# Weight products of three networks: one group of 512 tokens against two groups of 256 in the halves of a PSUM bank

## The chip, the cores and the metric

The kernel runs on one core of a Trainium2 chip. Its engines are TensorE (PE in the profile, with its weight loads as a row of their own, PEld), VectorE (DVE), ScalarE (ACT), GpSimd (POOL) and SyncE (SP), which issues most DMAs. The metric is the device time of one execution in microseconds, the median of several runs. The work is dense matrix products over 512 tokens, and nearly all of it stands on TensorE.

## The reference

Two transformer blocks follow each other on the same 512 tokens of 1,024 features. Between norms, attentions and gates stand three networks that this change touches:

```python
def swiglu(x, w1, w3, w2):
    return (jax.nn.silu(x @ w1) * (x @ w3)) @ w2
...
f = swiglu(rms_norm(h, ffn1_pre_g[l]), ffn1_w1[l], ffn1_w3[l], ffn1_w2[l])
h = h + 0.5 * rms_norm(f, ffn1_post_g[l])
...
f = swiglu(rms_norm(h, ffn2_pre_g[l]), ffn2_w1[l], ffn2_w3[l], ffn2_w2[l])
h = h + 0.5 * rms_norm(f, ffn2_post_g[l])
...
h2 = rmsnorm(x, g_mlp[i])
u = jax.nn.relu(jnp.einsum("bsd,df->bsf", h2, w_up[i]))
x = x + jnp.einsum("bsf,fd->bsd", u * u, w_down[i])
```

The first two have a hidden width of 2,816 (22 tiles of 128), the third of 4,096 (32 tiles). All values are float32.

## The kernel before, in words

Everything is held with features on the 128 partitions and tokens along the free dimension: a feature tile is 128 x 512, and `h` is eight of them. To keep float32 precision, every operand of a product is split into a rounded high part and the remainder, and one product of two tiles is three matmuls into the same PSUM bank: high x high, high x low, low x high (`mm3`, line 290 of the profile issues all of them). So each matmul comes with a weight load of its own (`LDWEIGHTS`), 128 x 128.

`lin` (line 296) makes one output tile: it takes a PSUM bank from a rotation of two pools (`lg` with three banks, `mm` with two), and runs over the k input tiles, three matmuls each, with a moving operand as wide as `tok`: 512 columns for all tokens, 256 for a half. `A` and `B` are the two halves of the tokens, `ALL` is both.

A network works in chunks of hidden tiles: 4, 4, 4, 4 and 6 in the two of 22 tiles (`ffn`), 6, 6, 6, 6 and 8 in the one of 32 (`mlp`). For each chunk it makes the hidden tiles ("up"), then adds their share to the eight output tiles ("down", `down` calls `stream`, which calls `lin`). The first chunk's ups are plain products: four or five are issued for half the tokens at a time while the norm before is still being finished (`begin`), the rest over all tokens (`stream`). The later chunks' ups go through `fast`: two output tiles by two halves of the tokens are got from seven products in place of eight, and each of those matmuls has 256 columns. The downs run over all 512 tokens, except the last few outputs of a network's last chunk, which are issued by halves (`tail` in `stream`).

Nobody writes the order of the instructions by hand: the framework's scheduler fixes it for each engine ahead of time, so where a product waits for an operand, matmuls of the next products stand between in TensorE's queue. At the end of a `fast` stretch the last of the seven products of the last pair (`last`) adds into a bank that VectorE has to read first (line 741 in `ffn`, line 1385 in `mlp`), so it stands behind the first matmuls of the down that follows. The last hidden tiles of a chunk reach the down through ScalarE (line 510, the high part) and VectorE (line 511, the low part).

Of the kernel before, what the change touches and what calls it, by code (L numbers as in the profile page):

```python
# [56 lines left out]
HALVES = (A, B)  # L57
ALL = slice(0, S)
# [116 lines left out]
def width(tok):  # L175
    return tok.stop - tok.start


class Net:
# [116 lines left out]
    def lin(self, wt, xs, tok=ALL, bank=None):  # L296

        out = (bank or self.pm)()[:, : width(tok)]
        for k, x in enumerate(xs):
            self.mm3(out, wt[k], (x[0][:, tok], x[1][:, tok]), k == 0, k == len(xs) - 1)  # L300
        return out

    def begin(self, jobs, step, fill=()):
# [1330 lines left out]
```

## Time and profile before

| | |
|---|---|
| median of 3 runs | 2098.67 us (2090.48 to 2103.62) |
| profiled execution, its own time | 2091.38 us |
| its span, first to last instruction | 2089.6 us |
| TensorE busy (share of the span), matmuls | 2011.4 us (96%), 12,428 |
| weight loads busy | 1766.1 us (85%) |
| VectorE, ScalarE, GpSimd busy | 1544.4, 1101.7, 254.4 us |
| mean granted TensorE clock | 0.99 of full speed |

How to read it: the ends of matmuls in a trace are modelled, and matmuls overlap in the pipeline, so a matmul of 256 columns shows a length of 276 ns or more while the next one starts 113 ns after it. What a matmul costs in a stream is therefore read from start to start: the start of one merged row of the timeline to the start of the next, divided by the number of matmuls in the first. Where a matmul waited, the timeline says so behind its row ("0.88 <-ACT b L510": idle for 0.88 us, released by the ScalarE instruction of line 510 that wrote a tile `b`).

### The profile page before, as it was taken

Reading aid. Unit: us, or ns where it says so; the run is one execution under the profiler, and the core shown is the slowest. Engines: PE = TensorE matmul, PEld = TensorE weight load, DVE = VectorE, ACT = ScalarE, POOL = GpSimd, SP = SyncE. Lnnn points to the kernel's source line nnn. Section 1 sums busy time; section 2 is a strip of 40 time slices with the busy share of each in tenths; the row PEclk is TensorE's granted clock in tenths of the full one; section 3 lists DMA queues with packets and bytes.
Section 4 is the critical chain, followed back from the end, with each engine's and each line's share of the span. In section 5 each row is a group of like instructions: output and inputs, shape, how many; then the busy total and the mean of one; then the engine's idle time right before and its main releaser. Section 6 shows DMA issues by size and latency. Waiting matters only on the chain. (4 is left out here: it accounts for less than half of the span.)

```text
span 2089.6 us, 32337 instructions
## 1 busy us (share of the span) xinstructions
PE 2011.4 (96%) x12428; PEld 1766.1 (85%) x12428; DVE 1544.4 (74%) x2956; ACT 1101.7 (53%) x2052; POOL 254.4 (12%) x239
## 2 busy tenths in 40 slices
PE   8999999899999999999999998998999999999997
PEld 7899998778778888998999998776778888988997
DVE  7977786799775585587777869588987678666755
ACT  5644454673573454554445445467864436444752
POOL 2000002313331310040000003213100000000001
PEclk9999999899999999999999999999999999999999
DMA  5233333212222233221333342211112313323331
GB/s 163 91 112 97 106 107 122 71 61 91 91 71 95 77 120 103 93 70 51 113 110 102 106 141 72 66 41 51 41 41 81 114 31 122 99 89 104 112 101 41
DMA packets 66010, 186.43 MB, mean 89 GB/s; under 512 B 6976, under 2 KB 14144, under 8 KB 65856
## 3 DMA queue, kind: packets, MB, share of 16 engines
q1 hardware_dynamic: 63376, 180.97, 26.8%
q10 hardware_dynamic: 2448, 3.41, 0.5%
q8 instruction: 97, 1.59, 0.3%
q14 instruction: 57, 0.47, 0.1%
q0 software_dynamic: 32, 0.00, 0.0%
HBM read 182.25 MB, written 2.10 MB: 88 GB/s over the span
## 5 line engine op out<-in xcount | busy, mean ns | idle before, releaser
L290 PE MATMUL mm<-x,w 128*128 128x512 f32 (+1 forms) x2064 | 473.8, 379 | 0.0
L290 PE MATMUL mm<-b,w 128*128 128x256 f32 (+1 forms) x2625 | 448.6, 322 | 2.0 <-ACT b L510 1.8
L290 PEld LDWEIGHTS mm<-x,w 128*128 128x128 f32 x2064 | 364.0, 188 | 74.9 <-DVE v L1274 0.7
L290 PEld LDWEIGHTS mm<-b,w 128*128 128x128 f32 x2625 | 375.2, 188 | 48.9 <-ACT b L510 4.2
L252 ACT CAST w<-r 128x1024 fp32r<-128x1024 f32 (+2 forms) x256 | 229.8, 898 | 277.8 <-PE mm L290 118.0
L290 PE MATMUL lg<-x,w 128*128 128x256 f32 (+1 forms) x2460 | 348.6, 295 | 6.8 <-DVE t L1385 4.7
L253 DVE TENSOR_TENSOR w<-r,w 128x1024 fp32r<-128x1024 f32 (+2 forms) x254 | 267.8, 1055 | 116.3 <-ACT w L252 111.3
L290 PE MATMUL lg<-b,w 128*128 128x256 f32 (+1 forms) x1929 | 352.9, 334 | 0.0
L290 PEld LDWEIGHTS lg<-x,w 128*128 128x128 f32 x2460 | 315.9, 188 | 27.9 <-DVE t L1385 6.4
L290 PEld LDWEIGHTS lg<-b,w 128*128 128x128 f32 x1929 | 294.5, 188 | 42.1
L457 ACT CAST w<-r 128x1024 fp32r<-128x1024 f32 x147 | 154.6, 1053 | 138.1 <-PE lg L290 81.3
L458 DVE TENSOR_TENSOR w<-r,w 128x1024 fp32r<-128x1024 f32 x147 | 178.7, 1221 | 19.9 <-ACT w L457 19.4
L290 PE MATMUL mm<-x,u 128*128 128x256 f32 x756 | 108.1, 287 | 15.6 <-ACT x L513 7.1
L510 ACT CAST b<-t 128x512 fp32r<-128x512 f32 (+1 forms) x113 | 60.8, 539 | 112.5 <-DVE t L745 34.3
L290 PEld LDWEIGHTS mm<-x,u 128*128 128x128 f32 x756 | 96.9, 193 | 18.7 <-ACT x L513 7.5
L569 POOL TENSOR_TENSOR sh<-sh,sh 128x256 f32<-128x256 f32 x45 | 37.5, 834 | 502.8 <-ACT sh L563 499.9
L511 DVE TENSOR_TENSOR b<-t,b 128x512 fp32r<-128x512 f32 (+1 forms) x113 | 67.2, 596 | 26.3 <-ACT b L510 26.0
L569 POOL TENSOR_TENSOR sf<-sf,sf 128x256 f32<-128x256 f32 x28 | 23.3, 833 | 450.4 <-ACT sf L563 440.4
L563 ACT ACTIVATE sh<-h 128x256 f32<-128x256 f32 x128 | 49.9, 411 | 52.5 <-DVE h L630 22.7
L928 POOL TENSOR_TENSOR b<-b,rows 128x512 f32<-128x512 f32 x32 | 52.5, 1642 | 174.7 <-ACT b L926 174.7
L861 DVE TENSOR_TENSOR u<-tt,u 128x512 fp32r<-128x512 f32 x92 | 62.0, 684 | 9.9 <-ACT u L860 9.3
L290 PE MATMUL lg<-x,b 128*128 128x256 f32 x456 | 68.1, 291 | 0.0
(271 smaller groups left out, 2738.9 us busy)
## 6 DMA issues: line engine op xcount, KB each, us to landing
r<-in_ffn_w SPq DMA_DIRECT2D x86, 512.0 KB, 3.3
r<-in_w_in SPq DMA_DIRECT2D x64, 512.0 KB, 3.2
r<-in_ffn_w SPq DMA_DIRECT2D x68, 256.0 KB, 2.7
r<-in_w_up SPq DMA_DIRECT2D x32, 512.0 KB, 3.2
r<-in_w_down SPq DMA_DIRECT2D x32, 384.0 KB, 3.4
r<-in_ffn_w SPq DMA_DIRECT2D x16, 384.0 KB, 3.3
r<-in_w_out SPq DMA_DIRECT2D x8, 512.0 KB, 3.2
r<-in_xattn_w_k SPq DMA_DIRECT2D x8, 512.0 KB, 3.2
```

What stands on the lines that cost most here:

```text
L252: nc.scalar.copy(hi, raw)
L253: self.second.tensor_tensor(lo, raw, hi.bitcast(F32), op=OP.subtract)
L290: self.nc.tensor.matmul(ps, lhsT=lhsT, rhs=rhs, start=start, stop=stop, skip_group_check=on)
L457: nc.scalar.copy(hi, raw)
L458: nc.vector.tensor_tensor(lo, raw, hi.bitcast(F32), op=OP.subtract)
L510: nc.scalar.copy(hi, src)
L511: nc.vector.tensor_tensor(lo, src, hi.bitcast(F32), op=OP.subtract)
L563: nc.scalar.activation(t, x, AF.Square)
L569: eng.tensor_tensor(ts[0], ts[0], t, op=OP.add)
L861: nc.vector.tensor_tensor(lo, ps[:, :n], hi.bitcast(F32), op=OP.subtract)
L928: nc.gpsimd.tensor_tensor(t[:, tok], t[:, tok], r[:, tok], op=OP.mult)
```

## The change

`lin` looks whether it is called for all tokens within one of the three networks. If so it makes its output as two groups, one after the other: all k input tiles for tokens 0 to 255 into the first half of the bank, then all k tiles again for tokens 256 to 511 into the second half. The weights of each tile are loaded for each half. What reads the bank afterwards still reads all 512 columns at once. Everything else, attention and projections included, stays as it was.

```diff
     def lin(self, wt, xs, tok=ALL, bank=None):
 
         out = (bank or self.pm)()[:, : width(tok)]
-        for k, x in enumerate(xs):
-            self.mm3(out, wt[k], (x[0][:, tok], x[1][:, tok]), k == 0, k == len(xs) - 1)
+
+        halves = tok == ALL and self.phase in ("ffn1", "ffn2", "mlp")
+        for at in HALVES if halves else (tok,):
+            ps = out[:, at] if halves else out
+            for k, x in enumerate(xs):
+                self.mm3(ps, wt[k], (x[0][:, at], x[1][:, at]), k == 0, k == len(xs) - 1)
         return out
```

TensorE's queue has 12,146 rows before and 13,952 after. The scheduler sets the new matmuls in other places, and two of them matter.

The first place is TensorE's queue at the change from `fast` to the first down behind it in `mlp`. `mm_19060` (after: `mm_20314`) is the bank of the down's first output, the tiles `b` are parts of hidden tiles and `w` the weights, `lg_18929` (after: `lg_20183`) is the bank of the last `fast` product, which waits for VectorE. Before:

```order
L290 MATMUL lg_18929<-x_18568,w_18926 128x256
L290 MATMUL mm_19060<-b_18636,w_19055 128x512 [waits DVE_49]
L290 MATMUL mm_19060<-b_18637,w_19055 128x512
L290 MATMUL mm_19060<-b_18636,w_19056 128x512 [waits DVE_49]
L290 MATMUL mm_19060<-b_18638,w_19055 128x512
L290 MATMUL mm_19060<-b_18639,w_19055 128x512
L290 MATMUL mm_19060<-b_18638,w_19056 128x512
L290 MATMUL mm_19060<-b_18642,w_19055 128x512
L290 MATMUL lg_18929<-x_18507,w_18925 128x256 [waits DVE_49]
```

And with the change:

```order
L290 MATMUL lg_20183<-x_19786,w_20180 128x256
L290 MATMUL mm_20314<-b_19890,w_20309 128x256 [waits DVE_49]
L290 MATMUL mm_20314<-b_19891,w_20309 128x256
L290 MATMUL mm_20314<-b_19890,w_20310 128x256
L290 MATMUL mm_20314<-b_19892,w_20309 128x256
L290 MATMUL mm_20314<-b_19893,w_20309 128x256
L290 MATMUL lg_20183<-x_19689,w_20179 128x256 [waits DVE_49]
```

Seven matmuls of 512 columns stood ahead of the product that waits, now five of 256 do. There are eleven more such places. At eight of them the numbers are three of 512 before and five of 256 now; in the last chunk of each `ffn` four and seven; in that of `mlp` five and ten.

The second place is TensorE's queue at the first down of the first network, where the fourth hidden tile comes late. `mm_745` (after: `mm_841`) is the first output's bank, `b_157` and `b_158` are the high and low part of that tile. Before:

```order
L290 MATMUL mm_745<-b_153,w_740 128x512 [waits Activation_49]
L290 MATMUL mm_745<-b_154,w_740 128x512 [waits DVE_49]
L290 MATMUL mm_745<-b_153,w_741 128x512
L290 MATMUL mm_745<-b_157,w_740 128x512 [waits Activation_49]
L290 MATMUL lg_772<-b_145,w_767 128x512
```

And with the change:

```order
L290 MATMUL lg_880<-b_149,w_876 128x256
L290 MATMUL lg_880<-b_153,w_875 128x256
L290 MATMUL lg_880<-b_154,w_875 128x256
L290 MATMUL mm_841<-b_157,w_836 128x256 [waits Activation_49]
L290 MATMUL lg_880<-b_153,w_876 128x256
```

Nine matmuls of 512 columns of this down stood ahead of the wait for `b_157`; now seventeen of 256 do, nine of the first output's first half and eight of the second output's.

## Rows read from the trace of the kernel before

**Rows 1.** The page's first lines: busy time and share of the span by engine, and the granted TensorE clock in 40 slices of the span (tenths, 9 is 90% or more).

```profile
PE 2011.4 (96%) x12428; PEld 1766.1 (85%) x12428; DVE 1544.4 (74%) x2956; ACT 1101.7 (53%) x2052; POOL 254.4 (12%) x239
...
PEclk9999999899999999999999999999999999999999
```

**Rows 2.** What TensorE waited for in the first network (37 to 352 us), then in the third (1650 to 2030 us): the waiting line, the releaser, us in total, times, longest.

```profile
PE mm L290 <- ACT b L510: 0.9, 1, 0.9
PE lg L290 <- DVE t L741: 0.5, 1, 0.5
PE lg L290 <- ACT sh L474: 0.5, 1, 0.5
...
PE lg L290 <- DVE t L1385: 4.7, 4, 2.0
```

**Rows 3.** Timeline of TensorE in a down of the first network, 512 columns a matmul, 12 matmuls an output tile: start, us, engine, line, operation, count.

```profile
188.50 2.96 PE L290 MATMUL mm<-b,w 128*128 128x512 f32 x12
191.29 2.96 PE L290 MATMUL lg<-b,w 128*128 128x512 f32 x12
194.09 2.96 PE L290 MATMUL mm<-b,w 128*128 128x512 f32 x12
196.90 2.96 PE L290 MATMUL lg<-b,w 128*128 128x512 f32 x12
```

**Rows 4.** Timeline of TensorE over the first `fast` stretch of the first network, 256 columns a matmul, and the start of the down behind it; between the first row and the row at 119.95 us stand 312 matmuls.

```profile
84.59 2.88 PE L290 MATMUL mm<-b,w 128*128 128x256 f32 x24
87.31 1.52 PE L290 MATMUL lg<-x,w 128*128 128x256 f32 x12
...
118.59 1.52 PE L290 MATMUL lg<-x,w 128*128 128x256 f32 x12
119.95 0.85 PE L290 MATMUL mm<-b,w 128*128 128x512 f32 x3
120.64 1.67 PE L290 MATMUL lg<-x,w 128*128 128x256 f32 x12
```

**Rows 5.** The same view of a `fast` stretch of the third network; between the first row and the last one's start stand 144 matmuls.

```profile
1810.99 1.58 PE L290 MATMUL lg<-b,w 128*128 128x256 f32 x12
1812.41 2.99 PE L290 MATMUL mm<-b,w 128*128 128x256 f32 x24
...
1827.95 1.58 PE L290 MATMUL mm<-x,u 128*128 128x256 f32 x12
```

**Rows 6.** TensorE in the twelve `fast` stretches of the three networks, each from its first matmul to the first of the down behind it: us, busy us and matmuls (one or two that began just before are counted with each), granted clock, DMA share, GB/s. The stretches hold 324, 324, 324 and 492 matmuls of their own in each of the first two networks, and 240, 240, 240 and 324 in the third, 3,972 in all.

```profile
83.23:119.95 36.72, 36.72 (x325) 1.00 0.39 123
143.93:181.31 37.38, 37.28 (x326) 1.00 0.35 108
205.30:242.32 37.02, 37.02 (x325) 1.00 0.35 108
266.28:323.72 57.44, 56.79 (x494) 1.00 0.37 115
985.88:1022.60 36.72, 36.72 (x325) 1.00 0.43 136
1046.59:1084.74 38.15, 38.15 (x325) 1.00 0.33 105
1108.69:1145.69 37.00, 37.00 (x326) 1.00 0.34 109
1169.66:1226.99 57.33, 56.81 (x493) 1.00 0.36 115
1737.71:1764.92 27.21, 27.21 (x242) 1.00 0.49 154
1802.32:1830.78 28.46, 28.46 (x241) 1.00 0.37 116
1866.47:1893.94 27.47, 27.47 (x242) 1.00 0.36 117
1930.32:1967.31 36.99, 36.99 (x326) 1.00 0.31 96
sum 457.89, PE 456.62; mean PE 38.05
```

**Rows 7.** Timeline of TensorE where the first `fast` stretch of `mlp` ends and its down begins.

```profile
1764.92 1.78 PE L290 MATMUL mm<-b,w 128*128 128x512 f32 x7
1768.67 1.65 PE L290 MATMUL lg<-x,w 128*128 128x256 f32 x12 [1.97 <-DVE t L1385]
```

**Rows 8.** Timeline at the first down of the first network: the nine matmuls ahead of the wait, the ScalarE cast that they wait for, and the matmul that waited.

```profile
59.69 2.26 PE L290 MATMUL mm<-b,w 128*128 128x512 f32 x9
...
62.15 0.62 ACT L510 CAST b<-t 128x512 fp32r<-128x512 f32 x1 [1.88 <-POOL t L719]
...
62.82 0.50 PE L290 MATMUL mm<-b,w 128*128 128x512 f32 x1 [0.88 <-ACT b L510]
```

**Rows 9.** The page's DMA queues: those that carry instructions (packets, MB, share of 16 engines' span).

```profile
q8 instruction: 97, 1.59, 0.3%
q14 instruction: 57, 0.47, 0.1%
```

## The prediction

> **What bounds the kernel now.** I read the busy line of the page first: TensorE is busy for 96% of the span, VectorE for 74%, and the granted clock is at its upper level, 2.4 GHz, in all 40 slices [rows 1]. That busy share is modelled, so the next view is the list of what TensorE waited for inside the networks: 1.9 us in the first and 4.7 us in the third [rows 2]. TensorE's own stream is the bound there; what the change is worth is the time that a matmul takes from start to start, times their number, and what happens to those few waits. The third view is therefore the timeline, read from start to start.
>
> With 512 columns, a down of 12 matmuls per output goes 188.50, 191.29, 194.09, 196.90: 8.40 us for 36, **233.3 ns each** [rows 3]. With 256 columns there are two paces. In the first `fast` stretch 312 matmuls take 119.95 - 84.59 = 35.36 us, **113.3 ns each** [rows 4]; in a stretch of the third network 144 take 1827.95 - 1810.99 = 16.96 us, **117.8 ns each** [rows 5]. Both hold for many groups on end at the full clock, with the same sources and banks. The row of stretches tells how they mix: 27.47 us for 240 matmuls is 114.5 ns, 28.46 us for 240 is 118.6, and over all twelve it is 456.62 busy us for 3,972, **115.0 ns** [rows 6]. Two halves thus cost 226.6 ns at the one pace, 235.6 at the other and 230.0 in the mean, against 233.3 for the whole. Cutting a matmul in two is nearly free here, and that is the point of the case: the whole matmul of 512 columns carries more than twice what half a one does.
>
> **How many.** In each `ffn` the down has 8 outputs x 22 tiles x 3 = 528 matmuls, less those that were issued by halves already: 5 x 6 x 3 = 90 in the first, 4 x 6 x 3 = 72 in the second, so 438 and 456. The plain ups over all tokens are 8 jobs less the 4 or 5 begun by halves: 4 and 3 jobs x 24 = 96 and 72. In `mlp` the down has 8 x 32 x 3 = 768 less 3 x 8 x 3 = 72, so 696, and 2 ups x 24 = 48. Together 1,806, which is by how much TensorE's queue grows (13,952 - 12,146), so the change does what it says. They fill 1,806 x 233.3 ns = 421 us, a fifth of the span.
>
> **The sum.** *Pace.* 1,806 x (230.0 - 233.3) ns = -6.0 us. The ends are 1,806 x (226.6 - 233.3) = -12.1 us if all go at the fast pace, and 1,806 x (235.6 - 233.3) = +4.2 us at the slow one. I take the mean of the stretches since they use the same tiles and weights in the same networks, and are what the new streams run on from. The weight loads double with the matmuls, but they have run once per 256 columns in those stretches already, so their price is inside the pace. So is that of fetching more instructions; the queues that carry them use 0.4% of the DMA engines [rows 9], and 3,612 instructions on top of 2 x 12,428 of TensorE's [rows 1] do not change that.
>
> That first pace is where a rule and the trace part. The Trainium skill, "TensorE: Matmul & The Clock Gate", section "Back-to-back issue gap", gives the gap between isolated matmuls at full clock as N/2.4 ns plus a fixed 2.5 ns. By it a whole matmul would cost 215.8 ns, a half 109.2, and a pair 2.5 ns more than a whole: +4.5 us, an estimate from that page. The rows above show a larger gap for both, and not the same addition to each, so I keep to them.
>
> *What the rows do not show.* No matmul of 256 columns in these rows is known to write the second half of a bank. Both ends for it are again the two paces; I see no reason for a third.
>
> *Cover ahead of waits.* The scheduler put fewer microseconds ahead of the product that waits for VectorE at the end of a `fast` stretch. In the first down behind `fast` in `mlp` seven matmuls of 512 (1.63 us) stood there, and still the product waited 1.97 us [rows 7]; now five of 256 stand there (0.57 us). VectorE's end does not move, so the 1.06 us of work that was under the wait comes after it: **+1.1 us**. At two more places in `mlp`, and three in each `ffn`, it is three of 512 (0.70 us) against five of 256 (0.57), in the last chunk of each `ffn` four (0.93) against seven (0.80), in that of `mlp` five (1.17) against ten (1.14). In the first stretch the product starts 0.69 us after the three began [rows 4], so the wait ends about when the cover does, and the loss is at most 0.13 each: 10 x 0.13 + 0.03 = **+1.3 us**, or nothing where VectorE is early. At the first down of the first network nine of 512 (2.1 us) stood ahead of the wait for ScalarE, which lasted 0.88 us [rows 8]; now seventeen of 256 (1.95 us) do, so about +0.15 us, and as much in the second. Sum +2.7 us; the lower end is the 1.1 us alone. I take 2.5.
>
> *What costs nothing.* The bank is read once for all 512 columns as before, so VectorE and ScalarE do the same work. An output still takes 12 matmuls' worth of time (2.8 us) or more, the time in which its bank is read and the next weights are split. SP's and POOL's queues are unchanged in order. If that cover were gone, each of the 120 downs would wait for its weights; rows 2 has no such wait now, and TensorE gains only 0.04 us per output of 12.
>
> Together -6.0 + 2.5 = **-3.5 us**: from the profiled execution's own 2091.4 us to 2087.9. The median of the runs shown is 2098.7, 7.3 us above that execution, and the three runs lie 13 us apart. From the median the same step gives 2095.2. I put the forecast between the two, at **2091 us**.
>
> **The rivals.**
>
> *All at the fast pace.* If the long streams without a change of width stay at 113.3 ns, the pace gives -12.1 and with the 2.5 us it is -9.6: 2081.8 by the profile. For it: seven of the twelve stretches lie within 1.3 ns of it [rows 6]. Against: two hold the slow pace for most of their length, and nothing in the rows tells what picks it. Chance 0.17.
>
> *All at the slow pace, so slower.* The mechanism is a cost per matmul, not per column, in the new streams: at 117.8 ns a pair costs more than a whole, +4.2 us, and with the cover +6.7: 2098.1. The point from which it decides: with 2.5 us spread over 1,806 pairs (1.4 ns) the change turns to a loss when the mean pace of the halves is above (233.3 - 1.4)/2 = 116.0 ns. The stretches at 1046.59 and 1802.32 are above it (117.7 and 118.6 ns), the other ten are not (the longest two, at 116.5 and 116.7 with their waits, are at 115.5 without) [rows 6]. Chance 0.22. The rule of the page named above belongs here: its fixed 2.5 ns would give nearly the same time, 2091.4 + 4.5 + 2.5 = 2098.4, an estimate from that page.
>
> *The cover is lost at every start.* Each of the 15 downs begins with matmuls that stand ahead of late operands; if at each the wait grows by what it did at 1764.92 us (1.06 us), that is 16 us in place of 2.5: 2091.4 - 6.0 + 16 = 2101. For it: the halves reach the last hidden tile of the first half of the tokens after half the time. Against: the scheduler fills the queue there with the next outputs' halves, as the second place of the order shows. It decides if the hidden tile's cast ends later than the fill. Chance 0.07.
>
> *The gain is absorbed.* TensorE saves 0.04 us per output and then waits for VectorE, which ends when it ended before: 2091 to 2094. The waits of rows 2 are few, so chance 0.06.
>
> **Numbers.** My case has 0.48. Of 1.00, all cases priced here lie between -10 and +10 us, within 1% (21 us), which is about what a measurement of this kernel can tell from no change. I leave 0.07 for faster by more than that (the fast pace together with a stretch or a run that the three runs do not show) and 0.05 for slower by more (something in the bank's second half, or waits everywhere). The range takes the fast rival at its profile time less 4 us for the scatter of the runs, and the lost cover with 6 us of the 7.3 between profile and median: 2078 to 2107.
>
> **What would show it.** In the profile after: no matmul of 512 columns in the three networks, 1,806 more rows; in a down the rows of 24 starting 2.72 us apart (fast pace) or 2.83 (slow) in place of 2.80; about 3 us of wait for line 1385 at the first down behind `fast` in `mlp`; the other waits of rows 2 within 0.2 us of what they are. I am wrong if a down shows a third pace, if waits for ScalarE or VectorE appear inside the downs, or if TensorE's clock falls in them.

## The result, and the profile after

The change takes **2111.13 us** (median of 6 runs, 2108.44 to 2113.42) against 2099.18 for the kernel before (6 runs, 2090.48 to 2103.62): a ratio of 1.0062, 95% interval 1.0046 to 1.0078. A later session gave 2111.9 against 2094.94, 1.0082 (1.0062 to 1.0103). It is slower by 12 to 17 us, still within 1%, where the forecast was 2091 us and the range ended at 2107. The profiled execution took 2113.42 us against 2091.38.

The page's first lines, and the granted clock in 40 slices of the span, where a 9 stands for 90% or more. Its mean is 0.985, against 0.990 in the profile before:

```profile
PE 2026.8 (96%) x14234; PEld 1861.4 (88%) x14234; DVE 1543.8 (73%) x2956; ACT 1101.9 (52%) x2052; POOL 255.6 (12%) x239
...
PEclk9999999999999999989999999999999999999999
```

Against [rows 1] there are 1,806 matmuls more and 15 busy us more, with the other engines' work unchanged. What TensorE waited for in the third network (1655 to 2050 us; waiting line, releaser, us in total, times, longest):

```profile
PE lg L290 <- DVE t L1389: 3.7, 4, 1.5
PE mm L290 <- ACT b L514: 2.1, 1, 2.1
PE mm L290 <- ACT sh L478: 1.1, 1, 1.1
PE lg L290 <- ACT sh L478: 1.0, 1, 1.0
```

Lines lie four further down than before. The wait that [rows 2] showed, for line 1385, has become shorter, 4.7 to 3.7. Three waits for ScalarE are new, 4.2 us. In the second network the wait for `b` at the first down went from 0.9 us to 2.1, in the first from 0.9 to 1.0.

The clock falls inside the downs too. This is TensorE around the wait of 2.1 us at the first down of the second network, which ends at 978.29 us (stretch, us, busy us and matmuls, granted clock, DMA share, GB/s):

```profile
976.00:979.30 3.30, 1.16 (x10) 1.00 0.00 0
979.30:982.70 3.40, 3.40 (x18) 0.51 0.02 5
982.70:986.00 3.30, 3.30 (x30) 0.99 0.29 79
```

For 3.4 us behind the wait the clock is at its lower level, 1.2 GHz, and 18 matmuls stand where 30 do afterwards. At the first down of the third network the profile shows the same from 1730.3 us on, behind the wait of 2.15 us.

The new downs, in the timeline. First a down of the first network, then one of the third (start, us, engine, line, operation, count):

```profile
192.63 2.99 PE L290 MATMUL lg<-b,w 128*128 128x256 f32 x24
195.46 2.99 PE L290 MATMUL mm<-b,w 128*128 128x256 f32 x24
198.28 2.99 PE L290 MATMUL lg<-b,w 128*128 128x256 f32 x24
201.11 2.99 PE L290 MATMUL mm<-b,w 128*128 128x256 f32 x24
...
1799.59 4.24 PE L290 MATMUL mm<-b,w 128*128 128x256 f32 x36
1803.67 4.24 PE L290 MATMUL lg<-b,w 128*128 128x256 f32 x36
1807.75 4.24 PE L290 MATMUL mm<-b,w 128*128 128x256 f32 x36
1811.83 4.24 PE L290 MATMUL lg<-b,w 128*128 128x256 f32 x36
```

The upper group goes at 8.48 us for 72, 117.8 ns, the lower at 4.08 for 36, 113.3: the two paces of [rows 4, 5]. That part of the forecast stands, outside the stretches at the lower clock. The loss must be elsewhere, and the page's table of DMA issues shows something that the prediction did not ask about. Before (operand, queue, count, KB each, median us from issue to landing):

```profile
r<-in_ffn_w SPq DMA_DIRECT2D x86, 512.0 KB, 3.3
r<-in_w_in SPq DMA_DIRECT2D x64, 512.0 KB, 3.2
r<-in_ffn_w SPq DMA_DIRECT2D x68, 256.0 KB, 2.7
r<-in_w_up SPq DMA_DIRECT2D x32, 512.0 KB, 3.2
```

After:

```profile
r<-in_ffn_w SPq DMA_DIRECT2D x86, 512.0 KB, 3.6
r<-in_w_in SPq DMA_DIRECT2D x64, 512.0 KB, 3.6
r<-in_ffn_w SPq DMA_DIRECT2D x68, 256.0 KB, 2.7
r<-in_w_up SPq DMA_DIRECT2D x32, 512.0 KB, 3.6
```

The loads of 512 KB land 0.3 to 0.4 us later in the median, those of `in_w_in` too, which belong to the mixers that the change does not touch; those of 256 KB do not. So there are two suspects: the first downs, and the loads.

To place the loss I read one matmul in every timeline, the first transposition behind the third network (tile `tt` from `ident` and `r`); what follows it takes 64 to 65 us in all kernels that do the whole work and have no tail appended. Before it starts at 2027.40 us, with the change at 2049.62: the 22 us between the two profiled executions are all in front of it.

### The profile page after: what moved, and what is told of

Read it like the earlier page. It is cut to its first block, busy times and chain, and to the rows that moved or that the text cites. A ratio compares the mean times of both kernels' runs of the same rounds, so it can differ in the third digit from the quotient of the medians.

```text
span 2111.6 us, 35966 instructions
## 1 busy us (share of the span) xinstructions
PE 2026.8 (96%) x14234; PEld 1861.4 (88%) x14234; DVE 1543.8 (73%) x2956; ACT 1101.9 (52%) x2052; POOL 255.6 (12%) x239
## 3 DMA queue, kind: packets, MB, share of 16 engines
q8 instruction: 111, 1.82, 0.4%
## 5 line engine op out<-in xcount | busy, mean ns | idle before, releaser
L290 PE MATMUL mm<-b,w 128*128 128x256 f32 (+1 forms) x3441 | 453.8, 286 | 6.0 <-ACT b L514 5.3
L290 PEld LDWEIGHTS mm<-b,w 128*128 128x128 f32 x3441 | 423.3, 189 | 16.7 <-ACT b L514 7.1
L290 PEld LDWEIGHTS mm<-x,w 128*128 128x128 f32 x2160 | 369.0, 188 | 71.5 <-DVE v L1278 0.7
L290 PEld LDWEIGHTS lg<-x,w 128*128 128x128 f32 x2580 | 323.4, 188 | 21.5 <-DVE t L1389 4.5
L290 PEld LDWEIGHTS lg<-b,w 128*128 128x128 f32 x2703 | 332.0, 188 | 6.2
```

The lines of the kernel that those rows point to most:

```text
L290: self.nc.tensor.matmul(ps, lhsT=lhsT, rhs=rhs, start=start, stop=stop, skip_group_check=on)
```

## The experiments

Three theories at the start. **Pace:** the new streams fell on the slow pace. **Cover:** at the first downs the halves use up what hid the late casts. **Loads:** the program's length makes loads slower (formed after the first runs, and later narrowed to the length of TensorE's own queue).

### The kernel before, again

No edit; a second trace of the same program.

> The kernel before, once more, for a second profile of it. It says how far two executions of one program differ stretch by stretch. Theory P (pace: which of the two paces, 113.3 or 117.8 ns, a stretch of 256-column matmuls takes is settled anew in each execution) expects fast stretches that change their pace between the two profiles of before, by up to 4.5 ns x 336 = 1.5 us each, and 5 to 10 us over the whole. Theory C (cover: the loss sits in waits at fixed places) expects the same paces and times within 2 us.

Measured: 2094.91 us in its one profiled run, loads of 512 KB as before, the transposition at 2030.46. So one profiled execution of the kernel before lies 3 us from another (61 runs of it, in five later sessions, lie between 2088.70 and 2103.15 us). The long `fast` streams change their pace between them: 19% of the matmuls of 256 columns in the `fast` stretches go at the slow pace in the first trace, 37% in this one, at the same places of the same program (counted start to start, the border at 115.6 ns). The paces are settled anew, as theory P said, but that moves the whole by 3 us, not by 5 to 10.

### Halves in one part alone, or in another order

Two runs have the diff of the change with a flag that `down` or the first ups set:

```diff
-        halves = tok == ALL and self.phase in ("ffn1", "ffn2", "mlp")
+        halves = tok == ALL and self.split_now
...
+            self.split_now = self.phase in ("ffn1", "ffn2", "mlp") and k0 > 0
```

`k0 > 0` are the downs behind a `fast` stretch (1,254 matmuls cut), `k0 == 0` in the other run the first chunk's ups and first downs (552).

> Halves only in the downs behind a fast stretch (1,254 of the 1,806 matmuls); the first chunk of each network stays at 512 columns. Theory C puts the loss into the first chunk (+6.4 us there between the two profiles): here +0 to +3 us against before. Theory P puts it into the pace of the new and the old streams of 256 columns: here +6 to +10 us.

Measured: 2102.03 us (10 runs) against 2096.76, ratio 1.0038 (1.0023 to 1.0053). Seven runs lie at 2099.67 to 2103.07, three at 2108.83 to 2112.5, the profiled one among these; what parts them I cannot say. The last 1,210 whole matmuls of these downs, those behind the last product of each `fast` stretch, took 283.37 us; the same work in halves takes 281.48, 1.9 less. So they are faster, and yet the kernel is slower by 5 to 8 us, with the first chunks as before (131.27 us). That is what theory P forecast, but not for its reason. Its loads of 512 KB land in 3.5 us.

> Halves only in the first chunk of each network, its plain ups and its down (552 of the 1,806 matmuls). Theory C: +5 to +8 us against before, from waits of 1 to 2.3 us at the first downs. Theory P: 552 x at most 2.3 ns = +1.3 us or less.

Measured: 2101.9 us (12 runs), ratio 1.0026 (1.0016 to 1.0037), with loads at 3.2 us. The stretch of plain ups and first downs of the three networks takes 137.00 us against 131.27: 5.7 more, as much as the whole loss by the ratio (5.5). (The profiled execution itself is 7 to 10 us behind the two of the kernel before, so some of that stands elsewhere.) With the change the same stretch takes 137.65 us, and 135.57 in a second trace. Waits for `b` at the first downs are 1.0, 2.1 and 2.2 us, as with the change.

The third keeps all the halves but lets both halves of a tile follow each other:

```diff
         for k, x in enumerate(xs):
-            self.mm3(out, wt[k], (x[0][:, tok], x[1][:, tok]), k == 0, k == len(xs) - 1)
+            for at in HALVES if halves else (tok,):
+                ps = out[:, at] if halves else out
+                self.mm3(ps, wt[k], (x[0][:, at], x[1][:, at]), k == 0 and not (halves and at == B), ...)
```

> All 1,806 in halves as in the change, but the two halves of an input tile stand next to each other (three matmuls for the first half, three for the second, then the next tile), so the late last tile is reached after as much work as before. Only the first matmul of a bank opens its group. Theory C: the waits at the first downs go back to those of before and the time to before's, -2 to +2 us. Theory P: the time stays at that of the change, +9 to +13 us against before.

Measured: 2111.99 us (6 runs), 1.0075 (1.0059 to 1.0092), as slow as the change. The wait for `b` at the first down of the third network is only 0.3 us here, since the early tiles' second halves stand ahead of the late tile again; in the second network it is 2.0. The stretch of first downs is 3.4 us shorter than with the change. The loads land in 3.6. So the first downs alone do not explain the loss, and the time is not that of before, as theory C had it.

### Does a longer program make loads slow, and which engine's?

The first try lengthens GpSimd's queue by 3,600 instructions, which is about what the change adds:

```diff
+            if self.phase == "ffn2" and c == 8:
+                self.idle(f[0][:, 0:1], 1500)
...
+            if c == 12:
+                self.idle(h[0][:, 0:1], 2100)
```

> The kernel before with 3,600 one-column memsets more on GpSimd, in two stretches of the second and third network where it has nothing to do; TensorE, VectorE, ScalarE and SyncE keep every instruction in its place. It makes the program as much longer as the change does and alters nothing else. Theory D (in the profiles of the change, of the pairs and of the downs alone, loads of 512 KB land after 3.5 to 3.6 us everywhere in the program, against 3.2 us in the others, and what the longer program displaces is the cause): 3.5 us or more here as well, and +4 to +8 us. Theory P and theory C: 3.2 us, and the time of before, -1 to +1 us.

Measured: 2213.43 us, a time that says nothing: the additions took longer than GpSimd's idle time, and the networks' ends waited for it (TensorE for 92.7 us at one place). But its loads of 512 KB land in 3.2 us, with 35,939 instructions in all against the change's 35,966. The length of the whole program is not it. (The page carries TensorE's instructions on the queue q8, [rows 9]: 1.59 MB here too.)

> The change once more, for a second profile of it on this chip. If the slower loads belong to the program (theory D), 512 KB land in 3.5 to 3.6 us again; if they belong to an execution or a chip, in 3.2 us in some. +11 to +15 us against before under every theory. Theory P expects other paces in the stretches than in the first profile; theory C the same waits at the first downs, 2.0 to 2.3 us each in the second and third network.

Measured: the change a second time, 2111.9 us, loads of 512 KB at 3.6, 3.5 and 3.5, the transposition at 2046.30. The late loads belong to the program, not to one execution.

Then TensorE's queue: the kernel before with every instruction in its place, and 1,806 products of one column behind the last of them, where no work of the kernel is left to be delayed.

```diff
         self.begin([], step)
+        ps = self.pa()
+        for _ in range(1806):
+            nc.tensor.matmul(ps[:, 0:1], lhsT=self.end[:, 0, 0:P], rhs=self.ones, start=True, stop=True)
```

> The kernel before, every instruction in its place on every engine, with 1,806 matmuls of one column more at the very end of TensorE's queue, behind the last output (so the whole time says nothing; the first 2,080 us are compared). TensorE's instruction queue then carries as much as with the change. Theory D' (loads land later because TensorE's part of the program is longer, wherever the instructions stand): 512 KB land in 3.5 us or more, and the stretches that the change does not touch lose 4 to 7 us against the two profiles of before. If it is the halves themselves that slow the loads: 3.2 us, and the same times within 3 us.

Measured: 2874.82 us with a tail of 780 that has no meaning, and loads at 3.7 us. The transposition starts at 2043.34, 15.9 us behind the first trace of the kernel before and 12.9 behind the second, with nothing altered ahead of it: more than the 4 to 7 us expected. The tail came out longer than meant, since each product becomes two matmuls, so this queue is longer than that of the change.

### The change between kernels with less work

To see whether the halves cost anything apart from the loads, both kernels with one of the three products left out in the mixers, the cross attention and the last gate (`mix`, `cross`, `mix2`, `ple`):

```diff
+        two = self.phase in ("mix", "cross", "mix2", "ple")
         mm(a[0], b[0], first, False)
-        mm(a[0], b[1], False, False)
-        mm(a[1], b[0], False, last)
+        mm(a[0], b[1], False, last and two)
+        if not two:
+            mm(a[1], b[0], False, last)
```

> The kernel before, leaving out the third product (low x high) of every weight product in the two mixers, the cross attention and the gate network, none of which the change touches. It shortens TensorE's program by some 1,400 matmuls. The control of the next run: 250 to 320 us less than before.

> The change, leaving out the same products as the run above, so that TensorE's program is hardly longer than that of before. Theory D': loads of 512 KB land in 3.2 us, and against the control the change costs only what stands in the networks without slower loads, +2 to +6 us. Without D': +11 to +15 us against the control, and 3.5 us or more if the halves slow the loads.

Measured: 1974.26 us without the halves and 1972.38 with them: with less work elsewhere the change looks 1.9 us faster, where 2 to 6 slower was expected. (Leaving out the products saved 121 us, not 250 to 320.) But it is the kernel without the halves that has loads that land late now (3.6 us, its TensorE instructions 1.41 MB), and the one with them whose loads land early (3.2 us, 1.64 MB). A longer queue does not make loads later as such. The comparison had to be made again with lengths alike.

### Lengths made alike

The kernel with one product left out gets 905 of the one-column products behind its last instruction, and the kernel before, whole, gets 907. Each becomes two matmuls and two weight loads on TensorE, so 905 of them are as many instructions as 1,806 matmuls more with their loads, within a few.

> Whole matmuls, the low-by-high product left out in mix, cross, mix2 and ple as in the run before the last, and 905 products of one column behind everything else on TensorE, which bring its instructions to the number of the changed kernel with the same products left out. The time as a whole has no meaning, since the tail is in it (780 us for 1,806 of them earlier, so some 390 here); what counts is where the work stands up to the tail's start, and how long the loads of 512 KB take. Theory D' (the loads' landing time goes with the length of TensorE's instructions): 512 KB lands in 3.2 us as in the changed kernel of that pair, not in 3.5 to 3.6 as in its control, and the end of the third network comes 10 us or more earlier than in that control. Theory C (first downs wait behind late casts): with the loads alike the changed kernel of the pair is 3 to 6 us behind this one by then, most of it at the first downs. Rival: the halves cost nothing with loads alike, and the two are within 1.5 us.

> The kernel before, whole, with 907 products of one column behind everything else on TensorE, as many instructions of TensorE as the changed kernel has. Again only the part ahead of the tail counts. Theory D': 512 KB lands in 3.5 to 3.7 us as in the changed kernel, and the end of the third network comes 10 to 16 us later than in the profile of the kernel before, with no matmul of the work changed. Theory C: the changed kernel is then 3 to 6 us behind this one. If the loads land in 3.2 us here, the length alone does not set their time, and the 12 us of the change stay open between loads and halves.

The pages of these two, the queue of TensorE's instructions (packets, MB, share) and the first line of the DMA issues. With one product left out, then whole:

```profile
q8 instruction: 101, 1.65, 0.3%
...
r<-in_ffn_w SPq DMA_DIRECT2D x86, 512.0 KB, 3.2
```

```profile
q8 instruction: 112, 1.84, 0.3%
...
r<-in_ffn_w SPq DMA_DIRECT2D x86, 512.0 KB, 3.6
```

Both landing times are as expected, in opposite directions: the same kind of tail made the loads land earlier in one kernel and later in the other. All runs together:

| kernel | TensorE's instructions, MB | `in_ffn_w`, 512 KB, us | transposition starts, us |
|---|---|---|---|
| before, first and second trace | 1.59 | 3.3, 3.2 | 2027.40, 2030.46 |
| GpSimd lengthened | 1.59 | 3.2 | no meaning |
| first chunks by halves | 1.67 | 3.2 | 2037.70 |
| downs of the third network by halves | 1.67 | 3.3 | 2035.45 |
| downs behind `fast` by halves | 1.75 | 3.5 | 2044.02 |
| change, first and second trace | 1.82 | 3.6, 3.6 | 2049.62, 2046.30 |
| both halves of a tile in turn | 1.82 | 3.6 | 2048.66 |
| before, as long as the change | 1.84 | 3.6 | 2039.87 |
| before, longer | 2.06 | 3.7 | 2043.34 |
| less work, before | 1.41 | 3.6 | 1921.61 |
| less work, change | 1.64 | 3.2 | 1919.07 |
| less work, before, as long as the change | 1.65 | 3.2 | 1914.36 |

The transposition in the kernel before at the change's length, and in the change:

```profile
2039.87 0.38 PE L593 MATMUL tt<-ident,r 128*128 128x128 f32 x2
```

```profile
2049.62 0.38 PE L597 MATMUL tt<-ident,r 128*128 128x128 f32 x2
```

By the profiled executions the 22.2 us part into 12.5 for the length, with its late loads (2027.40 to 2039.87; 9.4 from the second trace of before), and 9.7 for the halves (to 2049.62; 6.4 in the second trace of the change; theory C expected 3 to 6). Executions of one kernel scatter by more than 3 us, so I also take the median runs less the time from the transposition to the end in the same kernel's profile (64 us; 448.1 with the tail): before 2096.2 - 64.2 = 2032.0, before at the change's length 2485.9 - 448.1 = 2037.8, change 2111.9 - 64.0 = 2047.9 (two sessions, between which the kernel before differs by 1 us). That is **6 us for the length and 10 for the halves**. For the kernels with less work the same sum gives 1919.7 for late loads, 1914.0 for early loads and 1918.2 for the halves with early loads: again 6 for a length with late loads (7 by the profiles, where 10 or more was expected), and **4 for the halves**. The tail is assumed to be as long in the median run as in the profiled one, and the kernels with a tail were run four times each, so these are good to a few us, and 10 and 4 may be the same.

What the length costs is not time in which TensorE waits. Here is all of TensorE up to the transposition: the two traces of the kernel before, the kernel before at the change's length, and the two traces of the change (stretch, us, busy us and matmuls, granted clock, DMA share, GB/s):

```profile
0.00:2027.40 2027.40, 1960.62 (x12004) 0.99 0.28 91
0.00:2030.46 2030.46, 1967.90 (x12004) 0.99 0.27 91
0.00:2039.87 2039.87, 1976.40 (x12005) 0.98 0.29 90
0.00:2049.62 2049.62, 1976.25 (x13811) 0.99 0.29 90
0.00:2046.30 2046.30, 1973.89 (x13810) 0.98 0.29 90
```

TensorE is idle for 66.8 and 62.6 us before, 63.5 at the change's length, 73.4 and 72.4 with the change. So the halves cost 9 to 10 us of waits. The length costs none: the same 12,004 matmuls take 8.5 to 15.8 us more. Most of that goes with the clock. These 24 matmuls are the same ones, behind a wait of 2.1 us before and of 1.9 at the change's length:

```profile
930.21 3.07 PE L290 MATMUL mm<-x,u 128*128 128x256 f32 x24
933.12 2.08 PE L290 MATMUL lg<-x,b 128*128 128x256 f32 x16
```

```profile
940.34 5.47 PE L290 MATMUL mm<-x,u 128*128 128x256 f32 x24
945.60 2.19 PE L290 MATMUL lg<-x,b 128*128 128x256 f32 x16
```

They take 2.91 us from start to start before, 121 ns each, and 5.26 at the change's length, 219 ns each. The granted clock over the matmuls around them is 0.96 (897.49 to 939.69 us) and 0.85 (905.63 to 951.67). Up to the transposition 67 and 88 matmuls of 256 columns start 211 to 216 ns apart before, which is 256 columns at 1.2 GHz, and 156 at the change's length. At some 100 ns each that is 7 to 9 of the 9 to 12 us. Over all runs the clock's mean points the same way: 0.987 for 61 of the kernel before and 0.984 for ten of the change. Whether the late loads bring the clock down, or something else that goes with the length, no run shows.

Where the halves cost it is read with the lengths alike. The plain ups and first downs take 131.26 us in the kernel before at the change's length, as without the tail, and 137.65 and 135.57 with the change: 4.3 to 6.4 of the halves' 6.4 to 9.7 us stand there. The timeline of TensorE at the first down of the third network, in the kernel before at the change's length:

```profile
1717.55 3.66 PE L290 MATMUL mm<-b,w 128*128 128x512 f32 x15
1721.04 3.67 PE L290 MATMUL lg<-b,w 128*128 128x512 f32 x15
1724.55 2.96 PE L290 MATMUL mm<-b,w 128*128 128x512 f32 x12
1727.35 0.39 PE L290 MATMUL lg<-b,w 128*128 128x512 f32 x1
```

And with the change:

```profile
1720.59 1.93 PE L290 MATMUL mm<-b,w 128*128 128x256 f32 x15
1722.36 1.93 PE L290 MATMUL lg<-b,w 128*128 128x256 f32 x15
1724.12 1.93 PE L290 MATMUL mm<-b,w 128*128 128x256 f32 x15
1725.89 1.93 PE L290 MATMUL lg<-b,w 128*128 128x256 f32 x15
1729.97 0.38 PE L290 MATMUL mm<-b,w 128*128 128x256 f32 x1 [2.15 <-ACT b L514]
```

Before, 41 matmuls of 512 columns stand between the last up and the first use of the sixth hidden tile, which is the last of the twelve of the third row: 41 x 233.3 ns = 9.6 us. With the change, 60 of 256 stand there, 7.1 us at 117.8 ns, since in each bank the second half is queued behind the first, and that wants the late tile. The cast of the tile ends 9.3 us after the cover begins in either kernel; these are ScalarE's rows of the cast, before at the change's length and with the change:

```profile
1726.20 0.62 ACT L510 CAST b<-t 128x512 fp32r<-128x512 f32 x1
```

```profile
1729.30 0.61 ACT L514 CAST b<-t 128x512 fp32r<-128x512 f32 x1
```

1726.82 - 1717.55 = 9.27 us, 0.3 less than the cover, and 1729.91 - 1720.59 = 9.32, 2.2 more than it. The cast's time is the same, so the shorter cover alone turned into a wait. And the wait costs more than itself where the clock falls behind it: 48.35 us for the first chunk of the third network in this trace, 47.02 in the second one, which has the same wait (2.16 us) and no fall. In the second network twelve matmuls of 512 were the cover (nine and three, 2.8 us), now seventeen of 256 (2.0).

Behind this first down the waits for `sh` appear in the change:

```profile
1758.99 2.88 PE L290 MATMUL mm<-b,w 128*128 128x256 f32 x24
1762.83 1.63 PE L290 MATMUL lg<-x,w 128*128 128x256 f32 x12 [0.96 <-ACT sh L478]
1765.57 1.65 PE L290 MATMUL mm<-x,u 128*128 128x256 f32 x12 [1.11 <-ACT sh L478]
```

ScalarE's copy of `sh` stands in its queue behind a cast that waits for a load:

```profile
1761.46 1.05 ACT L461 CAST w<-r 128x1024 fp32r<-128x1024 f32 x1 [4.35 <-DMA r<-in_w_up]
1762.41 0.37 ACT L478 COPY sh<-lg 128x256 f32<-128x256 f32 x1
```

The load that it waits for took 4.8 us to land, 4.9 in the second trace. In the run that cuts the first chunks alone, whose loads land early, the same load took 3.1, and only one of the two waits is there, 1.0 us. In the kernel before at the change's length, with late loads, it took 3.4, and neither wait is there. So both causes have a part in these waits; how they make this one load so late is not shown.

### The downs of the third network alone

The flag of the second group with `self.phase == "mlp" and k0 > 0`: 552 matmuls, as many as in the first chunks, at a place without late tiles.

> Halves only in the downs behind a fast stretch of the third network: 552 matmuls are cut, as many as in the run that cut the first chunks alone, so the program of TensorE has the same length as there. Theory D': 512 KB lands in 3.2 us as in that run, and the time is what the kernel before takes, less the pace (552 x about -2 ns = -1 us) and plus the shorter cover behind the fast stretches (0 to +2 us): a ratio between 0.999 and 1.001, against 1.0026 for the first chunks. Theory C: no first down is cut, so the wait for ScalarE at the first down of the third network is absent, as in the kernel before. Rival: the halves cost something in themselves, wherever they stand (in the run with all downs behind fast stretches the ratio was 1.0038 for 1,254): then 552 give about 1.0017 with loads of 3.2 us.

Measured: 2096.02 us (12 runs) against 2096.86 (17 runs), ratio **0.9994** (0.9981 to 1.0007). Its instructions are 1.67 MB and its loads land in 3.3 us:

```profile
q8 instruction: 102, 1.67, 0.3%
...
r<-in_ffn_w SPq DMA_DIRECT2D x86, 512.0 KB, 3.3
```

There is no wait for `b` at the first down of the third network here, against 2.2 us with the first chunks cut. Halves that have no late operand behind them and leave the loads as they were cost nothing here, and gain nothing that can be measured (4.0 us less to 1.5 more by the interval): in this trace 73% of them fell on the slow pace, and the downs took 0.9 us more, not less. No version was found that beats the kernel before.

## Why the prediction was wrong

The kernel was forecast 3.5 us faster and became 12 to 17 us slower. Two steps failed, the cover at the first downs and what was priced at nothing; the pace was too large besides. The start of the sum was off by 2 us only: from the median of 61 later runs of the kernel before, 2096.2, the same step gives 2092.7.

**Pace, -6.0 us: right in its rows, too large.** The long rows of the downs run at 113.3 and 117.8 ns, as forecast. But behind the last product of each `fast` stretch the twelve downs take 282.17 us with the change (282.30 in the second trace) against 283.37 for the same work: -1.2 us for 1,210 pairs, -1.0 ns a pair where the step had -3.3, so -1.8 us for all. The mix of the paces was taken from stretches of which one trace had 19% slow and the next 37%; in the new downs 39 and 41% are. At the starts of the downs, where several outputs take turns, some matmuls start 0.12 to 0.4 us apart; the long rows leave them out. With these starts, and without the waits, all 1,254 pairs take 311.9 and 312.0 us against 312.4. The Trainium skill, "TensorE: Matmul & The Clock Gate", section "Back-to-back issue gap", gives its rule for isolated matmuls; by it each pair would have been 2.5 ns dearer than the whole. These, each with its weight load, were 1.0 ns cheaper behind the starts.

**Cover ahead of waits, +2.5 us: the first step that failed, at the wrong places.** At the change from `fast` to a down, priced at +1.1 and up to +1.3, no loss can be told from the scatter: the waits for line 1385 are 4.7 and 2.7 us in the two traces of before, 3.1 at the change's length, 3.7 and 4.1 with the change. At the first downs the step had +0.15 for the first network "and as much in the second", and none for the third. The first came out so (0.9 to 1.0). The second lost 1.2, since twelve matmuls and not nine stood ahead there, and the third 2.1 where [rows 2] has no wait at all: a wait that does not exist in the profile was not looked for, though it was avoided by 0.3 us, by 41 of the matmuls that the change cuts. The 2.1 us of waits for `sh` behind it were in no step, nor was a fall of the clock. The first chunks came out 4.3 to 6.4 us longer, where the step had +0.3 for their downs; cut alone, with early loads, they made the kernel 5 us slower.

**What costs nothing: the second step that failed.** "So is that of fetching more instructions; the queues that carry them use 0.4% of the DMA engines [rows 9]" was an argument from a share of time. The queues still use 0.5%, but a kernel with as many instructions of TensorE and not one matmul changed is 6 us slower by medians and 9 to 12 by the profiles, with the loads of 512 KB landing 0.3 us later and more of its matmuls at the lower clock. The 6 us rest on the assumption on the tail; that the mechanism is the loads is not shown. Had the loads stayed early, the 4 us of the halves would have given 2100 to 2103, an estimate, and in the range; that would have been luck, since the sign of the change was wrong even so.

**The clock.** The prediction read [rows 1] as the upper level in all 40 slices. One slice there is an 8, and a 9 says only 90% or more: up to the transposition that trace has 34 us at the lower level, and the change has 55 and 61. Of the signs that the prediction gave for being wrong two came: waits for ScalarE inside the downs, and the clock falling in them.

**The rivals.** "The cover is lost at every start" had the mechanism and put it at 15 places with 16 us; it holds at two, with 3.3 us, the waits that follow and the falls of the clock. All fast, all slow and absorbed did not occur: both paces are there, and neither is most of the loss. That the change does not do what it says is excluded by the count, 14,234 - 12,428 = 1,806.

**What stays open.** Why the length of TensorE's queue moves the landing of the loads, and how a program with late loads comes to more time at the lower clock. It is not the length as such, since loads land late at 1.41 MB, early at 1.59 to 1.67, and late at 1.75 to 2.06; where the program's parts lie in memory would fit such a pattern, but no run here moved them by anything but length. Nor is it shown whether the halves cost more with late loads (10 us) than with early ones (4); two different kernels (with less work and whole) stand behind the two numbers, and each is good to a few us. With both halves of a tile in turn the first downs lose less, and the time is no better; with halves in the downs behind `fast` alone, three of ten runs lie 9 us above the others. Neither was followed up.

## What to carry to other kernels

Before cutting an instruction in smaller pieces, look not only at the waits in the profile but at the operands that arrive just in time: for each, count the work in front of it in time, before and after, against the time at which its producer ends. And where a change adds or removes thousands of instructions, compare the landing times of untouched loads in both profiles first; if they differ, give the kernel before the same length with a tail of idle products, and compare the two ahead of the tail, idle and busy time apart: busy time that grows with the same matmuls points to the clock or the pace, not to waits.

## What the runs showed of the hardware

- The landing time of loads of 512 KB, the median of one operand, is 3.1 to 3.4 us in some programs and 3.5 to 3.9 in others. Both programs that were traced twice kept their level, and instructions added to TensorE's queue moved it, in either direction, even where they are executed behind all loads. Loads of 256 KB land in 2.7 us in both, those of 384 KB in 3.1 to 3.4.
- A stream of matmuls of 256 columns with a weight load each goes at 113.3 or 117.8 ns a matmul at the same granted clock, for tens of us on end, and the same place of the same program takes the one in one execution and the other in the next. Nearly all streams of 512 columns go at 233.3.
- Behind a wait of 2.0 to 2.1 us at the first down of the second network the granted clock fell to 0.5 of full speed, 1.2 GHz, in all five traces that have it, and in none of the nine with a wait of 0.8 to 0.9 us there. Behind one of 2.1 to 2.2 us in the third network it fell in two traces of four.
- 3,600 memsets of one column, put where GpSimd was idle, took longer than its idle time and cost the kernel some 118 us.
